# The first load of a transformer layer in two halves on two queues, with 20 instead of 24 warming products

## The chip, the cores and the metric

The kernel runs on one core of a Trainium2 chip. The metric is the device time of one execution in microseconds (us), as the median of several runs. In the profile PE is TensorE's products, PEld its weight loads, DVE is VectorE, ACT is ScalarE, POOL is GpSimd and SP is SyncE; a trailing q (SPq) is the engine's instruction queue, which also issues DMAs.

## What is computed

One layer with sliding-window attention, for 512 tokens of width 2048, followed by a gated embedding and two more norms, all in float32:

```python
hn = rmsnorm(x, norm_g[0])
q, k, v, gate = split(hn @ w_in)              # 2048, 256, 256 and 2048 columns
y = (swa(q, k, v, sinks, rel_bias) * silu(gate)) @ w_out
x = x + y                                      # 32 heads, 4 key heads, window 128
x = x + (p @ ple_proj) * sigmoid(rmsnorm(x, ple_norm) @ ple_gate)
return rmsnorm(x, final_g)
```

## The kernel before

Nearly all of the time goes into products with large weights on TensorE. Each float32 operand is split into a high part, rounded to the form that TensorE takes at full speed, and a low part, the rest. Three products (high by high, low by high, high by low) then stand for one; `mm3`, lines 126 to 128, writes them.

The work around the change is the start, a loop over the 16 chunks `k` of 128 of the 2048 input channels. Each chunk comes as one row block of the array `first`, 128 rows of 1281 columns: 256 tokens of the transposed x, one column with the norm's gain, 256 columns of the weights of the first two blocks of q, the other 256 tokens, and 512 columns of the weights of k and v. The tile that it lands in is `xw`. Chunks 0 and 1 come in two DMAs each, the others in one:

```python
parts = {0: (0, 2 * half + 1, XW), 1: (0, 3 * half + 1, XW)}.get(k, (0, XW))
for c0, c1 in zip(parts, parts[1:]):
    nc.sync.dma_start(xw[:, c0:c1], a["first"][k][:, c0:c1])
```

So the first piece of chunk 0 is 513 columns (half the tokens, the gain, the q weights) and the second is 768 (the other tokens and the k and v weights). All go out on SyncE's queue in the order of the code.

From `xw`, ScalarE makes `xh`, the high part of x times the gain (`high`, line 226), and VectorE makes `xl`, the low part (`low`, line 229). The weights are split in the same manner into `w0s` (lines 236 and 239). For chunk 0 the halves of the tokens are done apart: the first half needs the first piece alone, the second half the second piece. TensorE multiplies them into the sums for q (`qps`, line 273, six products for each half in chunk 0), k (`ktps`, lines 126 to 128) and v (`vps`, lines 286 and 288).

Before any data is there, TensorE runs `WARM` products of a tile of ones by itself (line 141) and two products of zeros that clear the sums of q (line 151). ScalarE takes the square root of a small tile `warm` (line 137), which loads its function table at a time when it has nothing else to do.

The order of the instructions of TensorE and SyncE is the order of the code throughout. In chunks 0 and 1 that holds for VectorE and ScalarE too. Each engine takes its instructions strictly in that order and waits at an instruction until the semaphores that it names have been raised.

Of the kernel before, what the change touches and what calls it, by code (L numbers as in the profile page):

```python
# [13 lines left out]
AF = mybir.ActivationFunctionType  # L14
# [6 lines left out]
P = 128  # L21
# [6 lines left out]
HB = P // 2  # L28
# [9 lines left out]
EPS = 1e-6  # L38
MASKED = -3.0e38
TOEP = 384  # L40
WARM = 24
XW = S + 1 + 768


# [11 lines left out]
def trunk_kernel(ctx: ExitStack, tc: tile.TileContext, a: dict):  # L56
    nc = tc.nc
# [24 lines left out]
    def bank(name, tag):  # L82
        return others.get(tag, psum).tile([P, 512], F32, tag=tag, name=name)
# [50 lines left out]

    warm = const.tile([P, 1], F32, tag="one", name="warm")
    nc.vector.memset(warm, 1.0)
    nc.scalar.activation(warm, warm, AF.Sqrt)
    ones = nc.const_aps.tensor(1.0, [P, P], mybir.dt.bfloat16)
    warm_ps = bank("warm_ps", "o")
    for _ in range(WARM):  # L140
        nc.tensor.matmul(warm_ps[:, :P], ones, ones, start=True, stop=True)
# [53 lines left out]
    for k in range(KC):  # L195
# [17 lines left out]
        xw = start_pool.tile([P, XW], F32, tag="xw", name=f"xw{k}")  # L213
        parts = {0: (0, 2 * half + 1, XW), 1: (0, 3 * half + 1, XW)}.get(k, (0, XW))
        for c0, c1 in zip(parts, parts[1:]):
            nc.sync.dma_start(xw[:, c0:c1], a["first"][k][:, c0:c1])
        xr = xw[:, : 2 * (2 * half + 1)].rearrange("p (n c) -> p n c", n=2)[:, :, :half]
        g1 = xw[:, half : half + 1]
        w_at = {512: half + 1, 0: 3 * half + 1, 256: 4 * half + 1}
# [21 lines left out]
        if k == 0:  # L241
            first, second = slice(0, 1), slice(1, 2)
# [428 lines left out]
    for (nm, p), small in zip(SUMS, (7, 5, 6, 4, None, None)):  # L671
# [7 lines left out]
        for jj in range(2):  # L679
            for m in range(4):  # L680
                t = summed[nm, p, jj, m] = tc.dram_tile([P, WE], F32, name=f"{nm}_{p}_{jj}_{m}")
                first = {7: (1, 2), 5: (1, 1)}.get(p)
# [785 lines left out]
```

## Time and profile before

| What | Value |
|---|---|
| Time, median of 3 runs | 792.33 us (792.25 to 792.47) |
| Time of the profiled execution | 792.22 us |
| Its span in the profile | 790.4 us |
| TensorE busy in the span | 780.8 us (99%) |
| VectorE, ScalarE, GpSimd busy | 590.9, 517.3, 141.0 us |
| Data moved by DMA | 184.87 MB, mean 234 GB/s |

The span is what the profile sees of the execution; the time also holds some 1.8 us around it. The profile has a chain of waits, followed back from the last instruction to what released each step, and tables that give each group of instructions its count, its busy time and the idle time before it. All times in them count from the span's start. The end of a product on TensorE is modelled and includes its way through the array, so that products that follow one another overlap in the tables; their rate is read from their starts.

### The profile page before, as it was taken

The page shows a single profiled execution, that of the slowest core. Times are in us where ns is not written, and L with a number is a line of the kernel's source. Part 1 is how long each engine was busy: PE and PEld are TensorE (multiplying, and loading weights), DVE is VectorE, ACT ScalarE, POOL GpSimd, SP SyncE. Part 2 cuts the span into 40 slices and gives each one's busy share as a digit, 9 for nine tenths or more (in the row PEclk, how much of TensorE's full clock was granted, in tenths as well). Part 3 has the DMA queues.
Part 4 walks back from the last instruction along what each step waited for, and adds up shares of the span by engine and source line. Part 5 has one row for each costly group of instructions (what it writes and reads, how often), then busy time and mean ns, then how long its engine had stood idle before and what let it go on. Part 6 is the DMA issues. An engine that isn't in the chain of part 4 may idle for free.

```text
span 790.4 us, 11177 instructions
## 1 busy us (share of the span) xinstructions
PE 780.8 (99%) x3658; PEld 649.2 (82%) x3658; DVE 590.9 (75%) x1171; ACT 517.3 (65%) x1131; POOL 141.0 (18%) x252
## 2 busy tenths in 40 slices
PE   9999999999999999999999999999999999999995
PEld 7888888888888888888888888888888888888885
DVE  4537568877888678776777899778867757988896
ACT  6735368776877676766666654456699656656765
POOL 0030222333332313341333100000000120210000
PEclk9999999999999999999999999999999999999998
DMA  8787977999999989899878499667864996787633
GB/s 337 244 213 253 297 192 229 291 265 291 251 253 282 242 229 263 215 254 252 228 201 184 137 371 342 190 217 233 273 235 142 348 206 198 157 227 218 182 106 107
DMA packets 44618, 184.87 MB, mean 234 GB/s; under 512 B 6720, under 2 KB 7232, under 8 KB 39440
## 3 DMA queue, kind: packets, MB, share of 16 engines
q1 hardware_dynamic: 36480, 142.94, 52.0%
q0 software_dynamic: 8080, 41.22, 27.4%
q8 instruction: 29, 0.48, 0.2%
q14 instruction: 29, 0.24, 0.1%
HBM read 177.26 MB, written 62.97 MB: 304 GB/s over the span
## 4 chain that ended last, share of the span: by engine, by line
PE 98%; DMA 0%; DVE 0%; ACT 0%; issue 0%; ACTq 0%; SPq 0%; DVEq 0%
PE gps L126 7%; PE gps L127 7%; PE gps L128 7%; PE qps L126 7%; PE qps L127 7%; PE qps L128 7%; PE o L128 6%; PE g L128 6%; PE g L126 6%; PE o L126 6%; PE g L127 5%; PE o L127 5%; PE s L476 2%; PE o L584 2%; PE vps L286 2%; PE pt L544 2%
## 5 line engine op out<-in xcount | busy, mean ns | idle before, releaser
L730 DVE TENSOR_TENSOR blo<-braw,bhi 128x1024 fp32r<-128x1024 f32 x102 | 124.5, 1223 | 41.0 <-ACT bhi L729 40.5
L729 ACT CAST bhi<-braw 128x1024 fp32r<-128x1024 f32 x102 | 107.4, 1053 | 72.8 <-PE o L128 26.4
L126 PE MATMUL gps<-xh,whi 128*128 128x512 f32 x256 | 100.5, 393 | 0.0
L127 PE MATMUL gps<-xl,whi 128*128 128x512 f32 x256 | 100.0, 391 | 0.0
L128 PE MATMUL gps<-xh,wlo 128*128 128x512 f32 x256 | 99.8, 390 | 0.0
L126 PE MATMUL qps<-xh,whi 128*128 128x512 f32 x224 | 87.6, 391 | 0.0
L127 PE MATMUL qps<-xl,whi 128*128 128x512 f32 x224 | 87.5, 391 | 0.0
L128 PE MATMUL qps<-xh,wlo 128*128 128x512 f32 x224 | 87.2, 389 | 0.0
L110 DVE TENSOR_TENSOR wlo<-wraw,whi 128x1024 fp32r<-128x1024 f32 x60 | 74.3, 1239 | 13.1 <-ACT whi L109 12.4
L126 PE MATMUL g<-bhi,fhg 128*128 128x512 f32 x192 | 75.1, 391 | 0.0
L126 PE MATMUL o<-bhi,fho 128*128 128x512 f32 x192 | 74.8, 390 | 0.0
L128 PE MATMUL g<-bhi,flg 128*128 128x512 f32 x192 | 74.8, 389 | 0.0
L128 PE MATMUL o<-bhi,flo 128*128 128x512 f32 x192 | 74.7, 389 | 0.0
L127 PE MATMUL g<-blo,fhg 128*128 128x512 f32 x192 | 74.7, 389 | 0.0
L127 PE MATMUL o<-blo,fho 128*128 128x512 f32 x192 | 74.7, 389 | 0.0
L555 ACT CAST r<-pt 128x256 fp32r<-128x256 f32 x64 | 23.9, 373 | 74.6 <-PE pt L544 74.5
L556 DVE TENSOR_TENSOR r<-pt,r 128x256 fp32r<-128x256 f32 x64 | 27.1, 423 | 57.2 <-ACT r L555 56.9
L109 ACT CAST whi<-wraw 128x1024 fp32r<-128x1024 f32 x60 | 62.3, 1039 | 10.6 <-PE qps L127 5.9
L563 POOL TENSOR_SCALAR_AFFINE_SELECT own<-r 64x512 fp32r<-64x512 f32 (+1 forms) x48 | 34.4, 718 | 167.0 <-PE o L587 80.7
L491 POOL COPY t<-sinkb 128x2 f32<-128x2 f32 x64 | 41.2, 644 | 99.3 <-ACT pr L533 38.7
L128 PEld LDWEIGHTS gps<-xh,wlo 128*128 128x128 f32 x256 | 48.1, 188 | 10.3
L126 PEld LDWEIGHTS gps<-xh,whi 128*128 128x128 f32 x256 | 48.1, 188 | 8.9
(230 smaller groups left out, 1753.5 us busy)
## 6 DMA issues: line engine op xcount, KB each, us to landing
w_out<-in_w_out POOLq DMA_DIRECT2D x32, 512.0 KB, 8.1
wraw<-in_w_gate_in SPq DMA_DIRECT2D x32, 512.0 KB, 6.8
braw<-w_out SPq DMA_DIRECT2D x32, 512.0 KB, 4.7
wraw<-in_w_q SPq DMA_DIRECT2D x28, 512.0 KB, 7.3
braw<-in_ple_gate SPq DMA_DIRECT2D x24, 512.0 KB, 3.6
braw<-in_w_out SPq DMA_DIRECT2D x22, 512.0 KB, 4.3
xw<-in_first SPq DMA_DIRECT2D x14, 640.5 KB, 6.5
w_out<-in_w_out SPq DMA_DIRECT2D x16, 512.0 KB, 11.2
```

What stands on the lines that cost most here:

```text
L109: nc.scalar.copy(hi, raw)
L110: nc.vector.tensor_sub(lo, raw, hi.bitcast(F32))
L126: nc.tensor.matmul(ps, sh, mh, start=first, stop=False, skip_group_check=more)
L127: nc.tensor.matmul(ps, sh, ml, start=False, stop=False, skip_group_check=more)
L128: nc.tensor.matmul(ps, sl, mh, start=False, stop=last, skip_group_check=more)
L286: nc.tensor.matmul(v_ps[t], h[:, c], part_of(high_at, 256, 512), start=f, stop=e, skip_group_check=True)
L491: nc.gpsimd.tensor_copy(two(0, W + W - 1 if late else W, 1), sinkb[:, d : d + 1].unsqueeze(1).to_broadcast([P, 2, 1]))
L555: nc.scalar.copy(rh, src)
L556: nc.vector.tensor_sub(rl, src, rh.bitcast(F32))
L563: nc.gpsimd.affine_select(out=flat(own, rows), in_=flat(r, rows).bitcast(F32), pattern=[[0, 2 * GROUP], [sign, TQ]], compare_op=ALU.is_ge, ...
L729: nc.scalar.copy(hi, raw)
L730: nc.vector.tensor_sub(lo, raw, hi.bitcast(F32))
```

## The change

The first piece of chunk 0 comes in two DMAs of 64 rows each: rows 64 to 127 are issued by ScalarE, rows 0 to 63 by SyncE. The square root that loads ScalarE's table moves behind ScalarE's DMA. `WARM` is 20 instead of 24.

```diff
-WARM = 24
+WARM = 20
...
     nc.vector.memset(warm, 1.0)
-    nc.scalar.activation(warm, warm, AF.Sqrt)
...
         for c0, c1 in zip(parts, parts[1:]):
-            nc.sync.dma_start(xw[:, c0:c1], a["first"][k][:, c0:c1])
+            if k == 0 and c0 == 0:
+                for rows, queue in ((slice(HB, P), nc.scalar), (slice(0, HB), nc.sync)):
+                    queue.dma_start(xw[rows, c0:c1], a["first"][k][rows, c0:c1])
+                nc.scalar.activation(warm, warm, AF.Sqrt)
+            else:
+                nc.sync.dma_start(xw[:, c0:c1], a["first"][k][:, c0:c1])
```

ScalarE's first instructions of the program, with the semaphores that they wait for (`xw_139` is the tile of chunk 0, `xh_142` and `w0s_138` are made from it; a semaphore DMAHW is raised by a landing), before:

```order
L137 ACT_TABLE_LOAD
L137 ACTIVATE warm<-warm 128x1 [waits DVE_49]
L226 ACTIVATE xh_142<-xw_139 128x256 [waits DMAHW0_49]
L226 ACTIVATE xh_142<-xw_139 128x256 [waits DMAHW1_49]
L236 CAST w0s_138<-xw_139 128x256 x2
```

And now, where the same tiles are called `xw_134`, `xh_139` and `w0s_133`:

```order
L217 DMA xw_134<-in_first 64x513
L218 ACT_TABLE_LOAD
L218 ACTIVATE warm<-warm 128x1 [waits DVE_49]
L230 ACTIVATE xh_139<-xw_134 128x256 [waits DMAHW1_49,DMAHW0_49]
L230 ACTIVATE xh_139<-xw_134 128x256 [waits DMAHW2_49]
L240 CAST w0s_133<-xw_134 128x256 x2
```

A DMA issue stands ahead of the table load, and the first half of `xh` waits for two landings. SyncE's first DMAs, chunks 0 to 3 in order, before:

```order
L216 DMA xw_139<-in_first 128x513
L216 DMA xw_139<-in_first 128x768
L216 DMA xw_181<-in_first 128x769
L216 DMA xw_181<-in_first 128x512
L216 DMA xw_214<-in_first 128x1281
L216 DMA xw_245<-in_first 128x1281 [waits DMAHW1_49,DMAHW0_49,DVE_49]
```

And now:

```order
L217 DMA xw_134<-in_first 64x513
L220 DMA xw_134<-in_first 128x768
L220 DMA xw_178<-in_first 128x769
L220 DMA xw_178<-in_first 128x512
L220 DMA xw_211<-in_first 128x1281
L220 DMA xw_242<-in_first 128x1281 [waits DMAHW1_49,DMAHW2_49,DMAHW0_49,DVE_49]
```

The first issue has half the rows, the others stand where they stood, and the first DMA that reuses a tile (chunk 3, in the tile of chunk 0) waits for one landing more. On VectorE nothing moves; its first cast from the tile of chunk 0 waits for both halves too. TensorE's order differs by the four products alone.

## The prediction, made before the changed kernel had run

> **What bounds the kernel now.** I read the chain that ended last first, then the waits of TensorE over the whole span, then busy time by stretch, to see how much of the time the start can be. The page's chain, the waits of TensorE and of its weight loader, and the stretches (us, then busy time and instructions of PE, PEld, DVE, ACT, POOL, then the clock, the DMA share and GB/s):
>
> ```profile
> PE 98%; DMA 0%; DVE 0%; ACT 0%; issue 0%; ACTq 0%; SPq 0%; DVEq 0%
> PE warm_ps L141 <- PEq L1458: 0.8, 1, 0.8
> PEld qps L273 <- ACT xh L226: 1.0, 2, 0.7
> 0.00:5.45 5.45, 4.47 (x33) 3.60 (x33) 1.30 (x6) 2.56 (x5) 0.70 (x6) 1.00 0.63 210
> 5.45:100.00 94.55, 94.55 (x449) 79.47 (x450) 52.45 (x101) 47.19 (x85) 13.71 (x35) 1.00 0.86 273
> 700.00:780.00 80.00, 80.00 (x377) 67.18 (x376) 70.14 (x98) 53.86 (x78) 3.44 (x4) 1.00 0.56 175
> 780.00:785.00 5.00, 1.77 (x15) 1.57 (x14) 3.79 (x16) 2.89 (x6) 0.00 (x0) 1.00 0.01 5
> ```
>
> TensorE waits only at the start. From 5.45 us it is busy in 94.55 of 94.55 us, and so on through 780 us, before a tail on other engines. It is one rigid train: if it starts earlier or later, so does the end. The question is therefore what sets the 5.45. The first pieces of the chain in order of time (start, duration), and one later piece:
>
> ```profile
> 0.81 0.38 SPq L216
> ...
> 1.25 3.61 DMA xw<-in_first
> ...
> 4.88 0.52 ACT xh L226
> ...
> 5.45 1.03 PE qps L273 x6
> ...
> 9.24 1.39 PE qps L273 x6
> ```
>
> The load on this chain is not the first one. It is issued at 1.25 us, second on SyncE's queue, and ends at 4.86. The loads at the start, with KB and us from issue to landing, name the two:
>
> ```profile
> xw<-in_first SPq DMA_DIRECT2D x1, 256.5 KB, 2.8
> xw<-in_first SPq DMA_DIRECT2D x1, 384.0 KB, 3.6
> ```
>
> The first piece (513 columns, 256.5 KB) is issued at 0.81 and lands at about 3.6. The second (768 columns, 384.0 KB) is issued at 1.25 and lands at 4.85. The change touches the issue of the first and leaves the second as it is. The timeline shows what hangs on each (start, duration, engine, line):
>
> ```profile
> 0.81 1.28 ACT L137 ACT_TABLE_LOAD   x1 [0.81 <-PEq L1458]
> 0.85 2.72 PE L141 MATMUL warm_ps<-const-bfloat16-1.0 128*128 128x128 bf16 x24 [0.85 <-PEq L1458]
> 2.10 0.20 ACT L137 ACTIVATE warm<-warm 128x1 f32<-128x1 f32 x1
> 3.36 1.06 PE L151 MATMUL qps<-const-bfloat16-1.0,blank 128*128 128x512 bf16 x2
> 3.60 0.51 ACT L226 ACTIVATE xh<-xw 128x256 fp32r<-128x256 f32 x1 [1.30 <-DMA xw<-in_first]
> 4.17 0.80 PE L273 MATMUL qps<-xh,w0s 128*128 128x256 f32 x4
> 4.28 0.48 DVE L229 SCALAR_TENSOR_TENSOR xl<-xw,xh 128x256 fp32r<-128x256 f32 x1
> 4.81 0.51 PE L273 MATMUL qps<-xl,w0s 128*128 128x256 f32 x2
> 4.88 0.51 ACT L226 ACTIVATE xh<-xw 128x256 fp32r<-128x256 f32 x1 [0.77 <-DMA xw<-in_first]
> ```
>
> The first piece feeds ACT at 3.60, and with it the six products at 4.17 and 4.81, which are over at 5.32. The second feeds ACT at 4.88, and ACT had been idle for 0.77 us. Its 0.51 us end at 5.39, and TensorE goes on at 5.45.
>
> **The change, part by part.** *Four warming products fewer.* The 24 take 2.72 us with the last one's drain, so four take about 4 x 0.107 = 0.43 us (2.51 us from 0.85 to the start of L151 at 3.36, over 24, gives 0.105). L151 then starts at about 2.94 and TensorE is free of it 0.43 us sooner. Before, this end (3.36 + 1.06 = 4.42 with its drain) and ScalarE's (3.60 + 0.51 = 4.11) fell together, so an earlier first piece could not have been used without the cut. But the next link is the second piece: nothing at 5.45 moves through the cut. Term: 0.
>
> *The square root that loads ScalarE's table moves behind the new DMA issue.* The price of an issue is in SyncE's rows: two issues, the second alone, and the eight small ones of 16 rows each (minimum, median and maximum in ns):
>
> ```profile
> 0.81 0.85 SPq L216 DMA_DIRECT2D xw<-in_first  x2
> 1.25 0.41 SPq L216 DMA_DIRECT2D xw<-in_first  x1
> L304 SPq DMA_DIRECT2D sinkb<-in_sinks x8: 311/418/423, 31.6 to 35.0; - x8
> ```
>
> An issue takes about 0.41 us, whether for 16 rows or 128. So ScalarE issues until about 1.22, loads the table until 2.50, and is done with the square root at 2.71. It then waits for the first piece as before: 0.89 us of its 1.30 us of idle time are left over. If that cover went, the first half of xh would start late by the excess. Term: 0. For SyncE the same rows say that half the rows save no issue time. It keeps as many issues, and the second piece still goes out at 1.25.
>
> *The first piece on two queues, and what that does to the second.* This is the one open term. Two stretches of DMA work at the start, each 1 us long, from 1.6 and from 2.6 us, and the share of the 16 DMA engines that two queues have over the whole span:
>
> ```profile
> DMA packets 65, 0.13 MB, mean 133 GB/s; under 512 B 0, under 2 KB 0, under 8 KB 65
> DMA packets 150, 0.35 MB, mean 347 GB/s; under 512 B 16, under 2 KB 16, under 8 KB 150
> q1 hardware_dynamic: 36480, 142.94, 52.0%
> q0 software_dynamic: 8080, 41.22, 27.4%
> ```
>
> The first packets start at about 1.8 us (the busy line of that answer is empty before). At the speed of the second stretch the 0.13 MB would have taken 0.13 / 0.35 = 0.37 us, but they took 0.8: 0.43 us are lost while the engines get going. After that they run full. The second piece ends when 640.5 KB have gone through, whichever queue brings them; q0 and q1 are both counted against the same 16 engines. So its landing can move by what the split does to the 0.43 us: all of it won at best (-0.43), if two queues fill the engines where one leaves them waiting. At worst one issue is lost (+0.41), if ScalarE's issue has to be served ahead of SyncE's second. I take -0.1: the bytes ahead of it are unchanged, which speaks for 0, and the only stretch with room for a gain is the slow start, of which I count a quarter. The rows of the full-speed stretch are the nearest, and there is no room in them.
>
> Here the Trainium skill speaks against the change. The page "DMA: Bandwidth & Descriptors", section "Rules for kernel authors", says of two transfers to disjoint halves of the partitions "Don't bother": they serialize, since both halves spread over all 16 engines, packet by packet from two rings. By that rule the term is 0, the first piece lands no sooner and the sum is 792.33; by the slow start of the trace it could be as much as -0.43, 791.9. No row of this trace shows SyncE's and ScalarE's queues loading at once, so it cannot decide.
>
> *Downstream.* SyncE's fourth chunk now waits for one more landing, long past by then. If the train starts up to 0.43 us sooner, the second chunk must keep up:
>
> ```profile
> 6.61 0.72 ACT L226 ACTIVATE xh<-xw 128x512 fp32r<-128x512 f32 x1 [0.62 <-DMA xw<-in_first]
> 8.04 0.42 DVE L256 TENSOR_TENSOR w0s<-xw,w0s 128x256 fp32r<-128x256 f32 x1
> ```
>
> Its last operand for the products of L273 is there at 8.46, and the chain has them at 9.24: 0.78 us of room. Term: 0.
>
> Sum: 0 + 0 - 0.1 + 0 = -0.1 us. The profiled execution took 792.22 us (span 790.4, 1.8 around it), 0.11 below the median of 792.33. Against the median the sum is 792.2; against this execution it would be 792.1.
>
> **The rivals.** *A, the forecast: the split does not do what it says.* The second piece lands within 0.15 us of 4.85, and the first piece, sooner or not, only lengthens the wait for the second. For it: the chain, and the engines at full rate from 2.6 us. Against it: the 0.43 us of slow start. 792.2, between 792.1 and 792.4.
>
> *B: the two queues fill the slow start.* Both pieces land 0.2 to 0.43 us sooner. ACT starts the second half of xh at 4.45 to 4.68 and the train starts that much sooner: 791.9 to 792.1. Here the cut of four products would help only the first six, which are then waiting anyway.
>
> *C, the other side: ScalarE's half arrives late.* If the two issues are served one after the other, the half on ScalarE's queue comes up to 0.41 us later than now, while SyncE's queue already moves the second piece. The first half of xh then ends at 4.52 instead of 4.11 and the six products shift with it. They end at 5.32 by the modelled drain, 0.13 us before 5.45, so the delay decides from 0.13 us on, and at 0.41 it costs 0.28: 792.6. If the second piece comes 0.41 late as well, 792.7. For it: the issues on one queue stand 0.44 us apart. Against it: ScalarE has nothing else to do at 0.81.
>
> *D: TensorE stays at half rate.* Rows of 512 columns each, from the start and from later:
>
> ```profile
> 3.79 0.63 PE L151 MATMUL qps<-const-bfloat16-1.0,blank 128*128 128x512 bf16 x1
> 6.30 0.40 PE L126 MATMUL ktps<-xh,w0s 128*128 128x512 f32 x1
> 6.54 0.40 PE L127 MATMUL ktps<-xl,w0s 128*128 128x512 f32 x1
> ```
>
> The two products of L151 start 0.43 us apart (3.36, 3.79), those of L126 and L127 0.24. The rate doubles somewhere between 3.79 and 6.30, though the granted clock of the table of stretches reads 1.00 throughout. With 20 products TensorE is out of work from about 3.36 + 1.06 - 0.43 = 3.99 until the first piece lets it go on at 4.17. If this gap of 0.18 us (0.4 without the drain) made it begin again, the doubling would come 2.9 to 5.5 us after 4.17 instead of after 0.85. Taken at the middle, 8.4 us, the train runs at half rate for 2.9 us and loses 1.5: 793.8; at the earliest, 7.1, it loses 0.8: 793.1. For it: at 3.79 the rate was still half, so it hangs on work done before, and there is now less of it. Against it: the gap from 5.32 to 5.45, in which TensorE waited too, did not slow what follows, and the four runs of before lie within 0.25 us of each other, so what sets the doubling is not touchy. The Trainium skill, "TensorE: Matmul & The Clock Gate", Part 1, has the clock doubled after about 3.4 us of sustained activity, in a window that runs freely and does not start with the kernel. By that figure the loss would be about 1.1 us, an estimate from the page; the same section lets the clock fall back only after an idle window of about that length, by which a gap this short does not count.
>
> **How the numbers follow.** Chances: A 0.55, B 0.24, C 0.13, D 0.05, and 0.03 for what I have not seen. The likeliest is A, so 792.2. The range from 791.8 (B's best with 0.1 us of scatter, the runs before being 0.22 apart) to 792.8 (C's worst with the same) leaves out D and the unseen, and keeps a little of A to C back for scatter, so it holds about 9 in 10; cutting it to 8 would cut through B or C. A measurement of this kernel tells about 0.2% from no change, 1.58 us. B cannot reach that: even the 0.43 is 0.05%. On the slow side only D at its later end does. So faster 0.01, same 0.96, slower 0.03.
>
> **What the next profile would show.** The second half of xh (ACT, 256 columns) is the row to look at: at 4.7 to 5.0 A is right, at 4.45 to 4.68 B. The first half of xh says when the first piece landed; from 3.73 on C costs. The table load should end near 2.5 with ScalarE idle afterwards. TensorE should start its real train at 5.3 to 5.5, with 512-column products 0.23 to 0.24 us apart by 6.3; if they are 0.43 apart there, it is D. I am wrong if the train starts outside that, or if TensorE waits anywhere after it.

## The result, and the profile after

The changed kernel takes 794.08 us (median of 14 runs, 792.87 to 796.10), the kernel before 792.35 on the same chips. The ratio is 1.0025, with a 95% interval of 1.0017 to 1.0032. That is 1.7 us slower by the medians and 2.0 by the ratio. The forecast was 792.2, no change, in a range of 791.8 to 792.8. Five single executions among all runs took 1292 to 2045 us; the ratios and intervals leave them out, and without them no median moves by more than 0.2 us. The profiled execution took 793.55 us with a span of 791.8, 1.4 more than the span before.

The timeline of the kernel after, at the start (start, duration, engine, line, and in brackets the idle time before it):

```profile
0.81 0.56 ACTq L217 DMA_DIRECT2D xw<-in_first  x1
0.81 0.57 SPq L217 DMA_DIRECT2D xw<-in_first  x1
0.85 2.29 PE L140 MATMUL warm_ps<-const-bfloat16-1.0 128*128 128x128 bf16 x20 [0.85 <-PEq L1462]
1.40 1.28 ACT L218 ACT_TABLE_LOAD   x1 [1.40 <-PEq L1462]
2.94 1.06 PE L150 MATMUL qps<-const-bfloat16-1.0,blank 128*128 128x512 bf16 x2
4.14 0.51 ACT L230 ACTIVATE xh<-xw 128x256 fp32r<-128x256 f32 x1 [1.25 <-DMA xw<-in_first]
4.70 0.76 PE L277 MATMUL qps<-xh,w0s 128*128 128x256 f32 x4 [0.70 <-ACT xh L230]
5.85 0.51 ACT L230 ACTIVATE xh<-xw 128x256 fp32r<-128x256 f32 x1 [1.21 <-DMA xw<-in_first]
6.41 0.74 PE L277 MATMUL qps<-xh,w0s 128*128 128x256 f32 x4 [0.56 <-ACT xh L230]
```

Each of the two issues of 64 rows takes 0.56 to 0.57 us, where one of 128 rows took 0.38. ScalarE can start the first half of `xh` at 4.14 (3.60 before) and the second half at 5.85 (4.88 before). TensorE stands idle for 0.70 us ahead of its first products, and the train starts at 6.41 instead of 5.45.

The chain that ended last, and the loads at the start (KB, us from issue to landing):

```profile
1.44 4.39 DMA xw<-in_first
...
5.85 0.52 ACT xh L230
...
6.41 1.02 PE qps L277 x6
...
10.21 1.39 PE qps L277 x6
```

```profile
xw<-in_first SPq DMA_DIRECT2D x1, 384.0 KB, 4.4
...
xw<-in_first ACTq DMA_DIRECT2D x1, 128.2 KB, 2.7
xw<-in_first SPq DMA_DIRECT2D x1, 128.2 KB, 3.2
```

The chain runs through the same load as before, the second piece, but it goes out at 1.44 instead of 1.25 and takes 4.39 us instead of 3.61. Part of that is its own issue, a whole load of 128 rows behind the half:

```profile
1.44 0.82 SPq L220 DMA_DIRECT2D xw<-in_first  x1
```

It takes 0.82 us instead of 0.41 and is over at 2.26 instead of 1.66. The DMA engines stand half idle behind it: from 3.5 to 4.0 us they were busy for 53% and moved 172 GB/s, where before it was 98% and 387. The products of the second chunk start at 10.21 instead of 9.24. The waits of TensorE and the stretches (busy time of PE, PEld, DVE, ACT, POOL, then clock, DMA share and GB/s) show that nothing is won back behind that:

```profile
PE qps L277 <- ACT xh L230: 1.3, 2, 0.7
...
6.41:100.00 93.59, 93.59 (x445) 78.68 (x446) 51.57 (x99) 45.49 (x83) 13.51 (x35) 1.00 0.85 270
```

The start explains 0.96 of the 1.4 us. The rest is at the other end. The last store's issue, first of the kernel before and then of the kernel after, and its landing, which reads the same in both:

```profile
785.96 0.40 SPq L1414 DMA_DIRECT2D out<-x1s  x1
```

```profile
786.92 0.40 SPq L1418 DMA_DIRECT2D out<-x1s  x1
...
out<-x1s SPq DMA_DIRECT2D x1, 512.0 KB, 3.6
```

The store is issued 0.96 us later, as the train is. Before, the span ended at 790.4, 0.84 us behind its landing (785.96 + 3.6 = 789.56). Now it ends at 791.8, 1.28 us behind (790.52). So about 0.44 us were added after the last piece of work.

From these two traces came three theories, which the first expectations build on. The first: the two queues are served one after the other, which delays the landings. The second: TensorE's rate doubles late in some executions, since the gap is longer and the warming shorter. The third: one DMA more in the program lengthens the closing.

### The profile page after: what moved, and what is told of

Same layout as the page of the kernel before. It is cut to its first block, busy times and chain, and to the rows that moved or that the text cites. A ratio compares the mean times of both kernels' runs of the same rounds, so it can differ in the third digit from the quotient of the medians.

```text
span 791.8 us, 11173 instructions
## 1 busy us (share of the span) xinstructions
PE 780.6 (99%) x3654; PEld 648.8 (82%) x3654; DVE 590.8 (75%) x1171; ACT 517.0 (65%) x1131; POOL 140.9 (18%) x252
## 4 chain that ended last, share of the span: by engine, by line
PE 98%; DMA 1%; DVE 0%; ACT 0%; SPq 0%; issue 0%; ACTq 0%; DVEq 0%
PE gps L126 7%; PE gps L127 7%; PE gps L128 7%; PE qps L126 7%; PE qps L127 7%; PE qps L128 7%; PE g L126 6%; PE g L127 6%; PE o L126 6%; PE o L128 5%; PE o L127 5%; PE g L128 5%; PE s L480 2%; PE o L588 2%; PE vps L290 2%; PE pt L548 2%
```

## The experiments

Times are medians; before was 792.23, 792.26, 792.29, 792.36 and 792.28 us in the five batches (e, f, g, h1 and h2, h3 to h6).

### The two parts of the change apart

Twenty products alone (e1, in the kernel before):

```diff
-WARM = 24
+WARM = 20
```

> Only the 20 instead of 24 warming products; the loads as before. Theory 1 (the first loads on two queues are served one after the other, so the second piece lands about 1 us later) and theory 3 (one DMA more in the program puts the last store's landing first among the closing waits, 0.42 us) say that nothing in this kernel is different: 792.3 us, the train of products starts at 5.4 to 5.5 us. Theory 2 (with fewer warming products TensorE stays at half rate longer in some executions): 0.8 to 2 us slower in the median, 793.1 to 794.4, with runs 2 us or more apart.

Measured: 792.55, ratio 1.0002 (0.9993 to 1.0011). Its profiled execution, TensorE:

```profile
4.15 1.22 PE L273 MATMUL qps<-xh,w0s 128*128 128x256 f32 x4 [0.15 <-ACT xh L226]
5.17 0.63 PE L273 MATMUL qps<-xl,w0s 128*128 128x256 f32 x2
5.60 0.74 PE L273 MATMUL qps<-xh,w0s 128*128 128x256 f32 x4
```

The first four products take 5.17 - 4.15 = 1.02 us where before took 0.64 (4.17 to 4.81). So the rate was still half there, and the two behind them, 0.43 us for two, were no faster. That the four missing products put the doubling off is not shown: in f4 (below), with all 24 and the load as before, the first four products take 1.02 us too (4.07 to 5.09). It cost nothing that could be measured, and no run was above 792.83.

The profiles of e1, f2, f4 and h5 have the load of before unchanged. In them ScalarE starts the second half of `xh` at 4.54, 4.57, 4.45 and 4.60, as this row of f4 shows:

```profile
4.45 0.51 ACT L226 ACTIVATE xh<-xw 128x256 fp32r<-128x256 f32 x1 [0.44 <-DMA xw<-in_first]
```

So the 4.88 of the first profile, on which the prediction built, was the latest of five.

The split alone (e2, the changed kernel with `WARM = 24`):

```diff
-WARM = 20
+WARM = 24
```

> The split load on two queues as in the changed kernel, with 24 warming products. Theories 1 and 3: as slow as the changed kernel, about 794, the train starts at 6.2 to 6.5 us, runs spread over 2 us or more. Theory 2: the clock is what costs, so back to within 0.5 us of before (792.3 to 792.8), runs close together.

Measured: 793.68, ratio 1.0020 (1.0011 to 1.0030). The first half of `xh` starts at 4.18 and the train at 6.00. So the split, with its one DMA more, carries most of the loss, with 24 products too.

Both halves on SyncE, nothing on ScalarE (e3, in the kernel before):

```diff
-            nc.sync.dma_start(xw[:, c0:c1], a["first"][k][:, c0:c1])
+            for rows in (slice(HB, P), slice(0, HB)) if k == 0 and c0 == 0 else (slice(0, P),):
+                nc.sync.dma_start(xw[rows, c0:c1], a["first"][k][rows, c0:c1])
```

> The first piece in the same two halves, but both issued by SyncE, one after the other; 24 warming products, ScalarE issues nothing. If it is the second queue that costs (theory 1), this loses one more issue on SyncE's queue, at most 0.44 us, plus theory 3's 0.42 (one DMA more here too): 792.8 to 793.2, the second piece lands at 4.9 to 5.3. If it is the halving into 64 rows that costs, as much as the changed kernel: 794, second piece at 5.8.

Measured: 793.66, ratio 1.0022 (1.0013 to 1.0032), the same loss with one queue. SyncE's first three issues, each from its own window of the timeline:

```profile
0.81 0.58 SPq L217 DMA_DIRECT2D xw<-in_first  x1
...
1.45 0.57 SPq L217 DMA_DIRECT2D xw<-in_first  x1
...
2.07 0.59 SPq L217 DMA_DIRECT2D xw<-in_first  x1
```

The two halves take 0.58 and 0.57 us although nothing else issues, and the whole second piece behind them takes 0.59, where it took 0.41 before. So 64 rows are slow to issue on one queue as well, and the first theory falls as the one cause: no second queue is needed for a loss of this size. The way there differs, though. Here the second piece goes out at 2.07 and takes 3.3 us. In the changed kernel it goes out at 1.44 and takes 4.39.

The first half of `xh` comes at 4.44 here, and TensorE stands idle for 0.69 us ahead of its first products, behind 24 warming products:

```profile
5.00 0.76 PE L274 MATMUL qps<-xh,w0s 128*128 128x256 f32 x4 [0.69 <-ACT xh L227]
```

In this profile the rate had doubled by then: the four take 0.66 us (5.00 to 5.66), not 1.02. Of the nine executions behind the median (one of 1292 us left out) three took 794.4 us or more, which the section on the rate comes back to.

### The closing

e4 is the changed kernel with a later 1 MB load moved from SyncE to GpSimd, so that SyncE's and ScalarE's DMAs are as many as before:

```diff
-            nc.sync.dma_start(fg, a["final_g"].partition_broadcast(P))
+            nc.gpsimd.dma_start(fg, a["final_g"].partition_broadcast(P))
```

> The changed kernel, but with the load of the last norm's gain (at about 562 us, far from any limit) issued by GpSimd, so that the fast queues carry as many DMAs as before. Theory 3: 0.42 us faster than the changed kernel, about 793.6, and 0.9 us instead of 1.3 from the last store's landing to the end of the span. Without theory 3: 794.1 and 1.3 us. The start should be that of the changed kernel, the train from 6.2 to 6.5 us.

Measured: 796.22, ratio 1.0046 (1.0033 to 1.0058). The time is a miss and tells nothing of the count. GpSimd issued the load early, at 453 us, into the stage from 440 to 490 us, and TensorE's weight loader waited there:

```profile
PEld o L127 <- DVE blo L734: 2.6, 4, 1.1
```

The load fell into a stage of the train with little slack. Waits of 0.2 to 1.0 us in all on this line show in the profiles of eight other versions too; the train is not quite as rigid as the prediction had it. The closing itself did what was expected: the last store is issued at 789.03 and lands at 792.63, and the span ends at 793.5, 0.87 us behind, as before the change.

f4 is the kernel before with one load of 16 rows cut into two of 8, so that there is one DMA more and nothing else:

```diff
-            for h in range(GROUP):
-                nc.sync.dma_start(sinkb[QB * h : QB * h + QB], a["sinks"][h].partition_broadcast(QB))
+            for at, n in ((0, QB // 2), (QB // 2, QB // 2), *((QB * h, QB) for h in range(1, GROUP))):
+                nc.sync.dma_start(sinkb[at : at + n], a["sinks"][at // QB].partition_broadcast(n))
```

> The kernel before with one DMA more far from any limit: the first of the eight loads of the sinks at 32 us comes in two of 8 rows. Theory 3 (the last store takes the first instead of the last place among the semaphores that SyncE waits for at the end): 0.42 us slower, 792.6 to 792.7, and from the last store's landing to the end of the span 1.3 us instead of 0.9; the start is unchanged. Without theory 3: 792.2 and 0.9 us.

Measured: 792.65, ratio 1.0007 (0.9998 to 1.0015), 0.39 above before. In its profile the last store lands at 789.98 and the span ends at 791.3, 1.3 us behind, as in the changed kernel. The size is near the limit of the measurement in the medians, but not in the traces. The twelve profiles with as many DMAs as before end 0.84 to 0.96 us behind the landing of the last store. The eight with one more (the changed kernel, e2, e3, f1, f4, g2, g4 and h6) end 1.27 to 1.36 us behind it. SyncE's waits for DMAs in the closing, before and after, show why (in all, how many, the longest):

```profile
SPq L1464 <- DMA out<-x1s: 2.6, 3, 1.1
```

```profile
SPq L1468 <- DMA out<-x1s: 3.0, 1, 3.0
```

At the end SyncE waits for eight semaphores of DMAs one after the other. SyncE and ScalarE issue 320 DMAs before and 321 after, and they raise these semaphores in turn. With 320 the last store raises the last of the eight, so that its landing ends the last wait. With 321 it raises the first: one wait lasts until the landing, and the other seven follow it 0.06 us apart (790.58 to 790.94 in the changed kernel), which makes about 0.42 us. In all twenty traces the place of the last store among the eight and the length of the closing go together.

### The rate

The split with 32 warming products (f1, the changed kernel with `WARM = 32`), and the kernel before with 12 (f2):

```diff
-WARM = 20
+WARM = 32
```

> The changed kernel with 32 warming products, so that TensorE has no gap of work before the first piece (it is done with them and with L151 at 4.7 to 5.1 us, the first six products still end before the second piece is there). Theory 2 (a gap in TensorE's work at the start puts the doubling of its rate off, in some executions by several us): the spread of the changed kernel goes, 793.0 to 793.4 in the median and nothing over 794. Without theory 2: median 794 and a spread of over 2 us, as in the changed kernel.

```diff
-WARM = 24
+WARM = 12
```

> The kernel before, loads as they were, with 12 warming products: TensorE is out of work from about 3.0 to 4.15 us. Theory 2: the doubling comes after the train has started at 5.45, at 6.6 to 10 us, 0.6 to 2.3 us lost, about 793.6 in the median with a spread of about 2 us. Without theory 2: 792.2, spread about 1 us, as before.

Measured: 793.44, ratio 1.0015 (1.0006 to 1.0024), with no run of 11 above 793.98; and 793.67, ratio 1.0018 (1.0009 to 1.0027). Products of 512 columns in the profile with 12:

```profile
6.80 0.63 PE L126 MATMUL ktps<-xh,w0s 128*128 128x512 f32 x1
7.22 0.63 PE L127 MATMUL ktps<-xl,w0s 128*128 128x512 f32 x1
```

They start 0.42 us apart at 7.2 us, which is half the rate; before they were 0.24 apart at 6.3. TensorE had stood idle for 0.93 us ahead of its first product. So less warming alone, with the load as before, gives a loss of this size.

The changed kernel once more (g4):

> The changed kernel itself once more, for a second profile of its start and beside the others on one chip: 794.1 in the median, some executions over 795. If the profile falls on one of the slow executions, theory 2 says that products of 512 columns still start 0.43 us apart at 7 us and later.

Measured: 793.91, ratio 1.0020 (1.0012 to 1.0029). Its profile shows such an execution (794.55 us), which the first profile did not:

```profile
6.28 1.22 PE L277 MATMUL qps<-xh,w0s 128*128 128x256 f32 x4
...
7.73 0.63 PE L126 MATMUL ktps<-xh,w0s 128*128 128x512 f32 x1
8.15 0.63 PE L127 MATMUL ktps<-xl,w0s 128*128 128x512 f32 x1
```

The products stand 0.42 us apart until after 8 us. Of the 26 executions of the changed kernel, 12 took 794.4 us or more. Of the 43 executions of the four versions with the same split on the same two queues and 24 or 32 products (e2, f1, and g3 and h4 below), 2 did. And in e3, with 24 products but a gap of 0.69 us, 3 of 9 did. This speaks for the length of the gap and against the count of products as such.

### What in the split is slow

The rows whole, and three pieces by columns instead of two, all on SyncE (f5, in the kernel before; the sinks come in one load fewer, from rows repeated in the input's layout, so that the count stays):

```diff
-        parts = {0: (0, 2 * half + 1, XW), 1: (0, 3 * half + 1, XW)}.get(k, (0, XW))
+        parts = {0: (0, 2 * half + 1, 3 * half + 1, XW), 1: (0, 3 * half + 1, XW)}.get(k, (0, XW))
...
```

> A try for a faster one, on the chain of before: chunk 0 comes in three pieces on SyncE's queue, 513 columns, then the other 256 columns of x alone, then the 512 of the k and v weights (two of the sinks' loads are merged, from rows laid out in the input, so that the number of DMAs stays). The second half of xh waits for 384.5 KB instead of 640.5: at about 4.2 us instead of 4.85, the train from 4.8 instead of 5.45, and the k products at 5.8 if the weights are there by 4.9 and cast by 5.6. Best case 0.65 us faster, 791.6; if the third piece takes the place of the second (its casts end late), 0 to 0.3 us, 791.9 to 792.2.

Measured: 792.57, ratio 1.0004 (0.9995 to 1.0013), no gain. ScalarE has both halves of `xh` in one stretch from 3.57 on, but TensorE ran at half rate until about 6.4 us in the profiled execution, so the earlier data was not used. Later in that execution the weight loader waited 1.0 us in all on the line named at e4.

Two queues without a split of the rows: the whole first piece on SyncE, the whole second piece on ScalarE at the same time (g1, in the kernel before, the square root behind the load as in the change):

```diff
-            nc.sync.dma_start(xw[:, c0:c1], a["first"][k][:, c0:c1])
+            queue = nc.scalar if k == 0 and c0 else nc.sync
+            queue.dma_start(xw[:, c0:c1], a["first"][k][:, c0:c1])
...
```

> No halves: the whole first piece on SyncE's queue, the whole second piece (768 columns) on ScalarE's, both issued at once; 24 warming products, as many DMAs as before. If two issues at one time are served one after the other and ScalarE's comes first, as in the changed kernel, the pieces change places: the second lands first, at 3.8 to 4.2 us, and the first 0.4 us or more behind it, at 4.4 to 4.7, so that the train starts later by 0.3 to 0.6: 792.6 to 792.9. If the two queues share the engines from the start, both land at 4.4 to 4.9. If SyncE's comes first, the first lands at 3.6 to 3.9 and nothing is lost: 792.2.

Measured: 792.74, ratio 1.0005 (0.9997 to 1.0014). The issue on ScalarE, and the landings:

```profile
0.81 0.41 ACTq L216 DMA_DIRECT2D xw<-in_first  x1
```

```profile
xw<-in_first ACTq DMA_DIRECT2D x1, 384.0 KB, 3.6
xw<-in_first SPq DMA_DIRECT2D x1, 256.5 KB, 3.4
```

Two issues of 128 rows at once take the usual 0.4 us and neither waits for the other. The second piece lands at 4.41, as early as in any profile of the load of before; the first pays for it and lands at 4.21 instead of about 3.6.

The table load ahead of ScalarE's DMA (g2, the changed kernel with 32 products):

```diff
             if k == 0 and c0 == 0:
+                nc.scalar.activation(warm, warm, AF.Sqrt)
                 for rows, queue in ((slice(HB, P), nc.scalar), (slice(0, HB), nc.sync)):
                     queue.dma_start(xw[rows, c0:c1], a["first"][k][rows, c0:c1])
-                nc.scalar.activation(warm, warm, AF.Sqrt)
```

> The halves on two queues, but ScalarE loads its table first and issues its half after that, at 2.3 us, when SyncE's first issues are over; 32 warming products. If it is issuing at one time that costs, SyncE's issues are short again (0.4 us instead of 0.57), its second piece lands at 4.5 to 5.0 us, as before and 0.5 sooner than with 32 products and issues at once. The first piece is then late, at 4.4 to 4.9, waiting for ScalarE's half. If two queues are slow as such, the second piece lands at 5.4 or later here too. Time 793.0 to 793.4, of which 0.42 is the place of the last store's semaphore.

Measured: 793.37, ratio 1.0012 (1.0004 to 1.0021). It did not do what it was meant to:

```profile
0.81 1.28 ACT L216 ACT_TABLE_LOAD   x1 [0.81 <-PEq L1462]
0.98 0.55 ACTq L218 DMA_DIRECT2D xw<-in_first  x1
```

The DMA went out at 0.98, while the table was loading, so the two issues still overlapped. One thing changed: the issue of the second piece behind them took 0.57 us here (0.58 in g3, below), where it takes 0.82 in the six other profiles of the split on two queues. The second half of `xh` then starts at 5.00 (5.03 in g3), and at 5.44 to 5.96 in the six. What makes this issue take the one or the other time stays open.

The split with 32 products and as many DMAs as before (g3, the changed kernel with `WARM = 32` and the sinks in one load fewer):

> The changed kernel without its two by-effects: 32 warming products, and two of the sinks' loads merged so that the number of DMAs is that of before. What is left is the price of the split load alone, 0.5 to 0.9 us by theory 1: 792.8 to 793.1, that is 0.4 below the run with 32 products alone, with 0.9 us behind the last store's landing.

Measured: 792.79, ratio 1.0006 (0.9998 to 1.0015), 0.50 above before, where the same with one DMA more (f1) was 1.18 above. Of the difference of 0.68 the closing is 0.4 to 0.5: in their traces the last store is issued at 786.60 and 786.64, and the spans end at 791.1 and 791.6. The rest is scatter of the medians.

Now the split by columns instead of rows, on two queues, 128 rows each (h1); and by 96 and 32 rows (h2). Both with 32 products and the count as before:

```diff
-                for rows, queue in ((slice(HB, P), nc.scalar), (slice(0, HB), nc.sync)):
-                    queue.dma_start(xw[rows, c0:c1], a["first"][k][rows, c0:c1])
+                for n0, n1, queue in ((half + 1, c1, nc.scalar), (c0, half + 1, nc.sync)):
+                    queue.dma_start(xw[:, n0:n1], a["first"][k][:, n0:n1])
```

> The changed kernel with 32 warming products, as many DMAs as before, and the first piece halved by columns: 257 columns on SyncE, 256 on ScalarE, 128 rows each, where the split version beside it had 64 rows each. Theory (the form of 64 rows is what is slow): both issues take 0.38 to 0.41 us, SyncE's second piece goes out at 1.25, the first half of x lands by 3.7 and the second piece at 4.8 to 5.0; the train starts at 5.3 to 5.5 and the time is 792.2 to 792.5. Rival (any split in two costs it): the second piece lands at 5.0 to 5.5, the train starts at 5.9 to 6.1, and the time is 792.7 to 792.9.

```diff
-                for rows, queue in ((slice(HB, P), nc.scalar), (slice(0, HB), nc.sync)):
+                for rows, queue in ((slice(96, P), nc.scalar), (slice(0, 96), nc.sync)):
```

> The same, but halved by rows in the ratio of 96 on SyncE to 32 on ScalarE. Theory (any number of rows but the full 128 is slow to issue when a row is long): both issues take 0.5 us or more, the second piece lands at 5.0 to 5.5, the time is 792.7 to 792.9. Rival (the number of rows sets the issue time, fewer rows being slower): 96 rows issue in 0.40 to 0.50, 32 in 0.6 or more, and the second piece lands between 4.85 and 5.0.

Measured: 792.88, ratio 1.0003 (0.9994 to 1.0012), and 792.80, ratio 1.0004 (0.9994 to 1.0013). The issues took 0.38 and 0.40 us by columns, 0.39 (96 rows) and 0.42 (32 rows) by rows. The second half of `xh` started at 4.55 and 4.65, where the whole load has it at 4.45 to 4.88. So neither two queues nor a part of the rows is slow; 64 rows are. Nothing is gained by these splits either. The medians lie some 0.5 above before, though: with 32 products TensorE is free only at 5.27. Does that cost something by itself? The kernel before with 32 products (h5):

```diff
-WARM = 24
+WARM = 32
```

> The kernel before with 32 warming products and nothing else. Theory: TensorE is free at 5.27 and then has twelve products to run, so the products of the second chunk start 0.6 to 0.8 later than before and the time is 792.8 to 793.1; the versions with 32 products then owe their rest to these, not to the split. Rival (the extra products lie beside the loads): 792.2 to 792.4.

Measured: 792.43, ratio 1.0004 (0.9995 to 1.0013). The 32 products as such cost nothing that shows, against the expectation. The reason is in when the rate doubles. Two products of `xl` and the four behind them, by columns with 32 products (h1), then in the kernel before with 32:

```profile
5.93 0.59 PE L277 MATMUL qps<-xl,w0s 128*128 128x256 f32 x2
6.36 0.64 PE L277 MATMUL qps<-xh,w0s 128*128 128x256 f32 x4
```

```profile
5.08 0.40 PE L273 MATMUL qps<-xl,w0s 128*128 128x256 f32 x2
5.32 0.64 PE L273 MATMUL qps<-xh,w0s 128*128 128x256 f32 x4
```

The two take 0.43 us in the first (half rate) and 0.24 in the second (full rate), after the same 32 products. The moment of doubling moves by over a microsecond from one execution to the next, without any gap. In the profiled executions of h1 and h2 (spans of 791.6 and 791.3, 1.2 and 0.9 above before) it accounts for 0.77 and 0.84 us: TensorE had no idle time at the start, and its products for k begin at 7.07 and 7.14 instead of 6.30. The rest in h1 is a wait of 0.5 us on the line named at e4. What the 0.5 us of the medians consist of stays open; with medians that scatter by some 0.3 us they are not clearly apart from h5.

Last, without the confusion of the 32 products: by columns with 24 products and the count as before (h3), the same by 64 rows (h4), and the changed kernel with 96 and 32 rows as its only difference (h6). Their edits are those above.

> Halves by columns on two queues, 24 warming products, as many DMAs as before. Theory now (64 rows alone are slow to issue and late to land; 32 warming products cost by themselves, since TensorE is free only at 5.27): the second piece lands at 4.5 to 4.7, the train of the second half starts at 5.1 to 5.3, 0.2 to 0.3 earlier than before, and the time is 791.9 to 792.3. Rival (two loads at once cost something further on): the train starts as early, and the time is 792.5 or more.

> Halves of 64 rows on two queues, 24 warming products, as many DMAs as before: the price of the 64 rows alone. Theory: issues of 0.57, the second piece at 5.0 to 5.8, the train at 5.6 to 6.3, the time 792.6 to 793.2. Rival (the 64 rows cost nothing once TensorE is warm and the count is back): 792.2 to 792.4.

> The changed kernel as it is, 20 warming products and one DMA more, with 96 rows on SyncE and 32 on ScalarE. Theory: only the 64 rows and what they make of the gap fall away; issues of 0.39 and 0.42, the first piece at 3.8, a gap of TensorE of 0.3 to 0.4, one DMA more for 0.4: 792.4 to 793.0, and no execution above 793.6. Rival (TensorE stays at half rate with 20 products whenever the first piece comes in two): a third of the executions at 794.5 or above, median 793.3 to 794.

Measured, with as many DMAs as before: by columns 792.24, ratio 1.0000 (0.9991 to 1.0009); by 64 rows 792.97, ratio 1.0008 (0.9999 to 1.0017). The starts in the two profiles, columns first:

```profile
0.81 0.38 SPq L217 DMA_DIRECT2D xw<-in_first  x1
...
4.46 0.51 ACT L230 ACTIVATE xh<-xw 128x256 fp32r<-128x256 f32 x1 [0.56 <-DMA xw<-in_first]
...
5.14 0.64 PE L277 MATMUL qps<-xh,w0s 128*128 128x256 f32 x4
```

```profile
0.81 0.58 SPq L217 DMA_DIRECT2D xw<-in_first  x1
...
5.96 0.51 ACT L230 ACTIVATE xh<-xw 128x256 fp32r<-128x256 f32 x1 [1.22 <-DMA xw<-in_first]
...
6.51 0.74 PE L277 MATMUL qps<-xh,w0s 128*128 128x256 f32 x4 [0.57 <-ACT xh L230]
```

The same bytes on the same two queues: the train starts at 5.14 by columns and at 6.51 by 64 rows. In the medians the 64 rows cost 0.73 us against the columns. The interval of h4 just reaches no change, so the medians alone would not carry this; the starts do. In the nine profiles with 64 rows the second half of `xh` starts at 5.00 to 5.96, and in the nine others that show it as a row at 4.45 to 4.88.

The changed kernel with 96 and 32 rows (h6) took 792.57, ratio 1.0006 (0.9997 to 1.0014), 0.29 above before, and no run of 11 took over 793.29:

```profile
0.81 0.42 ACTq L217 DMA_DIRECT2D xw<-in_first  x1
...
0.81 0.39 SPq L217 DMA_DIRECT2D xw<-in_first  x1
...
3.80 0.51 ACT L230 ACTIVATE xh<-xw 128x256 fp32r<-128x256 f32 x1 [1.04 <-DMA xw<-in_first]
...
4.36 0.91 PE L277 MATMUL qps<-xh,w0s 128*128 128x256 f32 x4 [0.36 <-ACT xh L230]
```

The gap of TensorE is 0.36 us instead of 0.70, with the same 20 products, and the executions above 794 are gone. One number in the code, 64 instead of 96 and 32, carries 1.3 to 1.4 of the 1.6 to 1.7 us. The 0.29 us that are left are no more than the closing adds, which takes 1.3 us behind the landing here too. No version was measurably faster than before.

## Why the prediction was wrong, point by point

**The sum.** The loss has three parts. The 64 rows by themselves: 0.69 us (h4 against before; 0.73 against h3). One DMA more, at the closing: 0.42 in the traces, 0.39 in the medians of f4. And the late doubling, which the 64 rows bring about by the longer gap: nothing in about half of the executions and some 1 to 2 us in the others. In the median the last is 0.2 to 0.3 us (the changed kernel's 1.62 and 1.73 less the 1.45 of e2). Together they make 1.3 to 1.4 us, and 1.6 to 1.7 were measured; the difference is no larger than the scatter of the medians. In the prediction's sum the first stood at -0.1, the second was missing, and the third was a rival.

**"An issue takes about 0.41 us, whether for 16 rows or 128", and the second piece "still goes out at 1.25".** This step failed first. I drew a rule for 64 rows from issues of 16 and of 128. It was 0.57, the second piece went out at 1.44, and its own issue took 0.82. The trace of before had the row that would have warned of it, the issues of a transfer of 64 rows later in the program:

```profile
L438 SPq DMA_DIRECT2D DV<-diffs x12: 462/542/657, 105.4 to 152.2; - x12
```

Its median is 542 ns, and its smallest, 462, is above the largest of the 16-row issues quoted in the prediction, 423. It is a warning and no proof: copies of 512 KB in the same trace (L691) have medians of 474 to 592 ns.

**The split term, -0.1 within -0.43 and +0.41.** It measured +0.55 (e2), +0.96 (after) and +1.06 (h4) at the start of the train. In the changed kernel the second half of `xh` is 0.97 us late (5.85 instead of 4.88). The two issues are 0.60 of it: the issue of the second piece is over at 2.26 instead of 1.66. The other 0.37 come between the end of the issue and the landing, and what they are stays open. The upper bound allowed for one lost issue, 0.41, and for nothing behind it. The Trainium skill, "DMA: Bandwidth & Descriptors", "Rules for kernel authors", was right to speak against two halves of the partitions. Its reason, that they serialize and gain nothing, gives a loss of 0 and not the loss seen here. The split into 96 and 32 rows agrees with it: its second half of `xh` starts at 4.65 and 4.66, and the unsplit load has it at 4.45 to 4.88.

**Rival A, 0.55, rival B, 0.24.** A's landing within 0.15 us of 4.85 came in one of the nine profiles with 64 rows (g2, with 32 products); in the two of the changed kernel the second half of `xh` starts at 5.72 and 5.85. With another split (h1, h2, h3 and h6) the second half of `xh` starts at 4.46 to 4.66, inside the 4.45 to 4.68 that B named. That is no evidence for B: the unsplit load has it at 4.45 to 4.60 in four of its five profiles. The prediction's reading of the chain rested on the fifth. In two of the four (e1 and f4) TensorE, at half rate, had no idle time there, and its own products set the start of the train, at 5.60 and 5.52.

**Rival C, 0.13.** Its mechanism, one issue waiting for the other, shows in no trace: the two issues of 64 rows both start at 0.81 and take 0.56 and 0.57. Its consequence, the first half late and then the second, did come: SyncE's half landed 0.5 us behind ScalarE's (3.2 and 2.7 us after the issue). C priced the start of the train at 0.28 us for that, and it was 0.96.

**Rival D, 0.05.** Its mechanism is what happens in the slower executions (g4, f2). Its times, 793.1 to 793.8, came close to the whole by luck, since the whole holds two other costs. It was too small in my chances because the gap was worked out with the first piece landing at 3.60: 0.18 us. The gap became 0.70. With 0.15 and 0.36 us in the profile (e1, h6) no execution took 794.4 us or more, and with 0.32 and 0.37 (e2, h4) 2 of 21 did. With 0.68 to 0.70 (the changed kernel, g4, e3) it was 15 of 35. The profiles of the changed kernel have full rate with a gap of 0.70 and half rate with 0.68, so with such a gap it is the moment that decides. I argued against D from a gap of 0.13 us and from runs that lay close together, both of a kernel without the longer gap. The Trainium skill, "TensorE: Matmul & The Clock Gate", Part 1, has a window that runs freely, so that the doubling comes at another time in each execution; h1 and h5 agree, 6.4 us or so and before 5.1 after the same 32 products. The page puts the spread at 0.5 us to either side; here the two lie at least 1.2 us apart. That a gap needs a whole idle window to count is no safe reading where the rate has not doubled yet.

**"One rigid train".** The 0.96 us at the start did reach the last store unchanged. What was not looked at is what stands behind it: SyncE's closing, 0.44 us longer. One more DMA moves the last store from the last to the first of the eight semaphores that SyncE waits for at the end, and seven waits then stand behind it. f4 shows the cost, e4 and g3 take it away, and the traces show the waits. The prediction had no term for it.

**Four products fewer and the table load, both 0.** Both right: e1 is within the scatter, and ScalarE was idle for 1.25 us ahead of the first half of `xh`.

**The chances.** Slower by over 0.2% got 0.03. The measured 0.25% lies just beyond that bound, which three small costs of one sign reached together and none alone. The range allowed 0.1 us of scatter, from three runs 0.22 apart; the 33 executions of the kernel before in batch f run from 791.81 to 793.57.

## What to carry to other kernels

Price a DMA by a row of its own shape: the count of rows mattered here at 64 and not at 16, 32, 96 or 128. When a load at the start is changed, ask how long TensorE will stand idle ahead of its first products, since a gap of 0.7 us can throw away the warming that a gap of 0.4 us mostly leaves intact. And count the DMAs of the program: one more can cost at the very end, far from where it was added.

## What the runs showed of the hardware that was not expected

- A DMA of 64 rows of this load takes 0.55 to 0.58 us to issue on SyncE and ScalarE alike. The issue of 128 rows behind it on SyncE took 0.57 to 0.59 in three profiles (e3, g2, g3) and 0.82 or 0.83 in six. The first DMAs of 32, 96 and 128 rows take 0.38 to 0.42. Why 64 is slow stays open.
- Two queues issue 128 rows at the same time without a cost to either issue (g1, h3). Their loads share the engines: in g1 the first piece comes 0.65 us later than in before.
- The place of the last store among SyncE's eight closing waits is worth 0.42 us (all twenty traces).
- ScalarE's DMA goes out while its function table is loading: at 0.98 us, with the load running from 0.81 to 2.10 (g2).
- After the same 32 products TensorE's rate doubled at about 6.4 us in one execution and before 5.1 in another (h1, h5).
